# Three small edits to a one-core decoder layer: where the gating bias lies, when it is turned, and where a quarter of x2 is staged

## The chip, the cores and the metric

The kernel runs on one core of a Trainium2 chip. TensorE (PE) multiplies matrices and writes to PSUM banks. VectorE (DVE), ScalarE (ACT) and GpSimd (POOL) do the element-wise work. SyncE (SP) and POOL issue the transfers between the chip's memory (HBM) and the on-chip buffer (SBUF). Every engine works through its own instructions in order, and semaphores make one engine wait for another or for a transfer.

The metric is the device time of one execution in microseconds. For the kernel before, three runs gave 1558.74, 1558.91 and 1561.43 us; the median is 1558.91.

## The reference, cut to what matters

The program is one layer of a decoder with 512 positions and 2048 channels, all in float32:

```
h  = RMSNorm(x);  proj = h @ w_in          # q, k, v, gates, z_a, u, v, z_b, merge logits
o_a = sparse_attention(q, k, v) * silu(z_a)
u, v = split(gelu(uv))
o_b = u * (tril(w_s) @ LayerNorm(v) + b_s) * silu(z_b)      # gMLP gating, 8 groups, chunks of 128
merged = sigmoid(m_a) * (o_a @ w_up_a) + sigmoid(m_b) * (o_b @ w_up_b)
x2 = x + merged @ w_out
x3 = x2 + sigmoid(x2 @ w_ple_gate) * (p @ w_ple)
out = RMSNorm(x3) * final_g
```

Two pieces matter here. The first is `b_s`, the bias of the spatial gating, an array of 8 groups by 128 positions (`sgu_b`), together with the 8 matrices `w_s` of 128 by 128 (`sgu_w`); both must be transposed before the gating can use them. The second is x2, the layer's residual stream after the output projection: it is produced with positions on the partitions, and the next product, `x2 @ w_ple_gate`, needs it transposed, with channels on the partitions.

## The kernel before

**Precision.** Every float32 operand is split into a high part, made by ACT (`high`, line 142 or 144), and a low part, made by DVE (`low`, line 148 or 150). Each product is then three matmuls: high by high, high by low, low by high (lines 355 to 357, and 393 to 395 for the plain jobs). Activations are split once; weights are split as they stream in.

**Jobs, granules and units.** The matmul work is a list of jobs, one for each block of weight columns: `u`, `vn`, `zb`, `m0` to `m3` (columns of `w_in`), `ua`, `ub` (up projections), `wo0` to `wo2` (output projection), `pg0`, `pg1`, `pg3` (the last gate). The generator `gemm` walks through them. It stops after every unit of a few matmuls; `fill(n)` runs n units, and `finish(name)` runs to the end of a job. Four units make one granule: 12 matmuls of 512 columns that use up one split piece of the weights. At the start of a granule `gemm` runs the deferred work (`flush`), splits the weights for two granules ahead (`split_to`, with `state["ahead"]` at 2), and takes work off a background list (`pop`).

**Kind "S" jobs** compute two column blocks at a time by a scheme that trades one product for sums of the operands. It has seven products, named "1" to "7". The weight quarters b11 and b12 have four places each, the other two quarters go through the three places of `raw`. The high and low parts of S jobs lie in `hs` and `ls`, three places each. Job `u` runs its products in the order 1, 2, 5, 6 and 3 alternating, 7, 4, with 4 granules for each product; its product "1" uses small pieces from another pool, so `hs` is first used by product "2", from the fifth granule on. The four b11 places form a ring (`ring(i, ...)`, tags b110 to b113), which also serves other short-lived tiles in stages when no b11 is there.

**The pace of background work.** `state["pops"]` is added to a running sum at every granule, and each whole number reached takes one item off the background list. The fraction that is left is carried on through the rest of the program. After the gating's matrices have been turned, 64 items in four chunks (`oa_chunk`) are put on the list; they prepare the attention output for the up projection and must be gone when job `vn` ends. Later lists are four `sum_chunk`s during `wo0` and `wo1` (pace 0.7), `x2_chunk`s during `pg0` (0.8), and two `s4_chunk`s during `pg1` (0.5).

**The stage around the first edits.** When attention ends, the pools `quad` (b12, hs, ls, s1) and `mix` are opened on its memory. Line 1374 loads the two halves of `sgu_w`, line 1375 loads the bias `bn`, both on POOL's queue. After job `za7` come 12 units of `u`, the transpose of the bias on PE (`ps_b`, line 1491) and its copy on DVE (line 1492), 4 units, then for each half of `sgu_w` four transposes (`ps_w`, line 1497), a multiplication by the triangle (line 1498), a store to DRAM (line 1500) and 4 units.

**The stage around the third edit.** After `wo0`, its 512 columns of x2 are turned in two pairs of 128-column blocks (`turn_x2(0, ...)`, line 1729). For each block `stage` (line 1720) splits the transposed block into a tile named `x2t` and stores that to DRAM (`x2t_d`). `third_sum` (line 1698 onwards) takes a difference of halves through a tile `third` in `hs` and a tile `stage` in `ls`, and stores it as `s3x_d`. All this runs beside the matmuls of `wo1`, 8 units after each pair. Job `wo2`, the next S job, loads its b11 quarter into the ring.

## Time and profile before

| What | Value |
|---|---|
| median of three runs | 1558.91 us |
| the profiled execution, its own time | 1559.0 us |
| its span, first to last instruction | 1557.3 us |
| mean granted TensorE clock | 0.997 of full speed |
| PE busy | 1538.7 us, 99% of the span |
| DVE busy | 1195.3 us, 77% |
| ACT busy | 785.0 us, 50% |
| POOL busy | 252.8 us, 16% |
| HBM traffic over the span | 172 GB/s |

How to read the rows that follow. A timeline row has the start in us from the span's start, the duration in us, the engine, the line, the operation, the tiles it writes and reads (out<-in), the shapes and a count; a bracket at its end tells how long the engine stood idle before it and whose end released it. A row of waits tells the waiting instruction, whom it waited for, the time in total, how often, and the longest. A row of stretches has the stretch, its length, each engine's busy time with its count, the granted clock, the share of the DMA engines and GB/s. A DMA row ends with KB each and the time from issue to landing.

### The profile page before, as it was taken

To read this page: it belongs to the slowest core of one execution; us is meant where nothing else is said; L and a number is where in the kernel's file an instruction comes from. 1 tells how busy PE (TensorE), PEld (TensorE's weight loads), DVE (VectorE), ACT (ScalarE), POOL (GpSimd) and SP (SyncE) were. 2 spreads that over 40 slices of the span, in tenths; PEclk is the share of its full clock that TensorE was granted. 3 is DMA by queue.
4 is the path that set the end of the run, shared out by engine and by line. 5 is a ranking of instruction groups with operands and counts; after the bars stand their busy time and mean duration, and the time that the engine had idled before them with its cause. 6 is when DMAs were issued, how large, how long until landed. Compare 5 with 4: busy or idle time off the path is not lost.

```text
span 1557.3 us, 20518 instructions
## 1 busy us (share of the span) xinstructions
PE 1538.7 (99%) x7438; PEld 1288.9 (83%) x7438; DVE 1195.3 (77%) x1869; ACT 785.0 (50%) x1345; POOL 252.8 (16%) x413
## 2 busy tenths in 40 slices
PE   9999999999999999999999999999999999999997
PEld 8889988888887888888888888888888878888886
DVE  6547758888886888978887777777665677878877
ACT  6434446667664555555545444455323344544456
POOL 1201101101122342201121212210131221000000
PEclk9999999999999999999999999999999999999999
DMA  8436731213226894826473737674833478454665
GB/s 322 127 81 195 222 80 50 59 51 109 75 74 211 240 307 136 250 68 230 142 258 112 265 104 253 234 260 170 298 121 95 136 219 268 149 201 164 189 202 190
DMA packets 161429, 269.23 MB, mean 173 GB/s; under 512 B 9752, under 2 KB 80048, under 8 KB 158768
## 3 DMA queue, kind: packets, MB, share of 16 engines
q1 hardware_dynamic: 116240, 151.67, 31.0%
q0 software_dynamic: 44944, 116.00, 22.5%
q8 instruction: 58, 0.95, 0.2%
q14 instruction: 43, 0.35, 0.1%
q10 hardware_dynamic: 144, 0.26, 0.0%
HBM read 209.69 MB, written 58.20 MB: 172 GB/s over the span
## 4 chain that ended last, share of the span: by engine, by line
PE 94%; DVE 3%; DMA 1%; ACT 1%; issue 1%; POOL 0%; DVEq 0%; POOLq 0%; ACTq 0%
PE ps_m L355 7%; PE ps_m L357 7%; PE ps_m L356 7%; PE ps_t L1204 2%; PE ps_ub L394 2%; PE ps_ub L393 2%; PE ps_ub L395 2%; PE ps_za L381 2%; PE ps_za L382 2%; PE ps_za L383 2%; PE ps_pg L356 2%; PE ps_wo L355 2%; PE ps_pg L357 2%; PE ps_ua L356 2%; PE ps_ua L355 2%; PE ps_zb L356 2%
## 5 line engine op out<-in xcount | busy, mean ns | idle before, releaser
L148 DVE TENSOR_TENSOR ls<-b,hs 128x1024 fp32r<-128x1024 f32 x196 | 239.9, 1224 | 116.1 <-ACT hs L142 114.8
L142 ACT CAST hs<-b 128x1024 fp32r<-128x1024 f32 x196 | 206.0, 1052 | 231.2 <-PE ps_m L357 87.7
L148 DVE TENSOR_TENSOR lo<-raw,hi 128x512 fp32r<-128x512 f32 (+1 forms) x216 | 151.4, 706 | 82.5 <-issue 21.3
L142 ACT CAST hi<-raw 128x512 fp32r<-128x512 f32 (+1 forms) x216 | 129.3, 606 | 150.5 <-PE ps_ub L395 46.4
L142 ACT CAST hs<-raw 128x1024 fp32r<-128x1024 f32 x80 | 84.2, 1054 | 94.4 <-PE ps_m L357 35.5
L148 DVE TENSOR_TENSOR ls<-raw,hs 128x1024 fp32r<-128x1024 f32 x80 | 97.8, 1223 | 14.8 <-ACT hs L142 14.6
L355 PE MATMUL ps_m<-hs,act_h 128*128 128x512 f32 x256 | 100.5, 393 | 0.0
L356 PE MATMUL ps_m<-ls,act_h 128*128 128x512 f32 x256 | 99.7, 389 | 0.0
L357 PE MATMUL ps_m<-hs,act_l 128*128 128x512 f32 x256 | 99.6, 389 | 0.0
L258 DVE TENSOR_TENSOR b<-raw,b 128x1024 f32<-128x1024 f32 x80 | 97.5, 1219 | 1.9 <-DMA raw<-in_w_in_dram 1.3
L258 DVE TENSOR_TENSOR b<-b,b 128x1024 f32<-128x1024 f32 x80 | 97.5, 1218 | 0.0
L142 ACT CAST pth<-ps_t 128x512 fp32r<-128x512 f32 (+1 forms) x88 | 47.9, 545 | 65.8 <-PE ps_t L1204 65.5
L1165 ACT ACTIVATE prob<-prob,st 128x512 f32<-128x512 f32 (+3 forms) x128 | 70.7, 556 | 4.0 <-DVE st L1156 3.8
L148 DVE TENSOR_TENSOR ptl<-ps_t,pth 128x512 fp32r<-128x512 f32 (+1 forms) x88 | 56.2, 639 | 21.0 <-ACT pth L142 20.0
L1156 DVE CUSTOM_DVE_ANT_0 prob<-ps_s,b 128x512 f32<-128x512 f32 (+3 forms) x128 | 56.3, 486 | 10.0 <-PE ps_s L1153 9.7
L357 PEld LDWEIGHTS ps_m<-hs,act_l 128*128 128x128 f32 x256 | 48.1, 188 | 10.1
L355 PEld LDWEIGHTS ps_m<-hs,act_h 128*128 128x128 f32 x256 | 48.1, 188 | 9.7
L356 PEld LDWEIGHTS ps_m<-ls,act_h 128*128 128x128 f32 x256 | 48.1, 188 | 9.7
L381 PE MATMUL ps_za<-act_h,hi 128*128 128x512 f32 x128 | 55.8, 436 | 0.0
L381 PE MATMUL ps_q<-act_h,hi 128*128 128x512 f32 x128 | 53.6, 419 | 0.0
L394 PE MATMUL ps_wo<-lo,act_h 128*128 128x512 f32 x128 | 49.9, 390 | 2.2 <-DVE lo L148 2.2
L1204 PEld LDWEIGHTS ps_t<-ident,prob 128*128 128x128 f32 x320 | 39.7, 140 | 13.8 <-DVE ptl L148 2.8
(641 smaller groups left out, 4395.9 us busy)
## 6 DMA issues: line engine op xcount, KB each, us to landing
raw<-in_w_in_dram SPq DMA_DIRECT2D x112, 512.0 KB, 3.9
b<-in_w_in_dram SPq DMA_DIRECT2D x56, 512.0 KB, 5.3
raw<-in_w_out_dram SPq DMA_DIRECT2D x24, 512.0 KB, 3.8
raw<-in_w_ple_gate_dram SPq DMA_DIRECT2D x24, 512.0 KB, 4.4
raw<-in_w_up_b_dram SPq DMA_DIRECT2D x16, 512.0 KB, 3.7
hsum<-h_stage POOLq DMA_DIRECT2D x12, 512.0 KB, 4.1
gate<-keep POOLq DMA_DIRECT2D x24, 256.0 KB, 4.7
oa_d<-oa_g POOLq DMA_DIRECT2D x40, 128.0 KB, 3.4
```

Of the source, the lines that this page charges most:

```text
L142: nc.scalar.copy(hi, src)
L148: nc.vector.tensor_tensor(out=lo, in0=src, in1=hi.bitcast(F32), op=ALU.subtract)
L258: nc.vector.tensor_tensor(out=b[o], in0=b[x], in1=b[y], op=ALU.subtract)
L355: nc.tensor.matmul(o, ah, wh, start=st, stop=False, skip_group_check=go)
L356: nc.tensor.matmul(o, ah, wl, start=False, stop=False, skip_group_check=go)
L357: nc.tensor.matmul(o, al, wh, start=False, stop=sp, skip_group_check=go)
L381: nc.tensor.matmul(ps, hi[:, j], ah, start=st, stop=False)
L382: nc.tensor.matmul(ps, hi[:, j], al, start=False, stop=False)
L394: nc.tensor.matmul(o, ah[:, sl], lo[:, j], start=False, stop=False)
L1156: nc.vector.tensor_tensor_reduce(out=pt[:, j * n:j * n + n], in0=o[:, j], in1=b0[:, 512 - n:], scale=-SLOPE[h], scalar=3.0e38, op0=ALU.add ...
L1165: nc.scalar.activation(sl, sl, AF.Exp, bias=st[:, 0, j, hh:hh + 1], scale=-1.0, accum_out=st[:, 1, j, hh:hh + 1])
L1204: nc.tensor.transpose(b[:, (2 * e + hh) * P:(2 * e + hh + 1) * P], pts[hh][:, c:c + P], ident)
```

## The change

There are three edits.

1. The bias tile `bn` moves from the tag `s1` (two places, otherwise used for sums and for what product "1" leaves) to the tag `hs` (three places).
2. The bias is turned after 20 units of `u` instead of 12, so it and all that follows it in the program (the two halves of `sgu_w`, the start of the background chunks) come two granules later. The pace of the background goes from 1.3 to 1.33 items for each granule.
3. The four `x2t` tiles, one for each 128-column block of x2's first quarter, lie in the four places of the b11 ring instead of in `hs`.

```
-    bn = quad["pool"].tile([P, 2, 256], F32, tag="s1", name="bn", bufs=2).rearrange("p a s -> p (a s)")[:8, :P]
+    bn = quad["pool"].tile([P, 2, 256], F32, tag="hs", name="bn", bufs=3).rearrange("p a s -> p (a s)")[:8, :P]
...
-    state["pops"] = 1.3
-    fill(12)
+    state["pops"] = 1.33
+    fill(20)
     b = bank("o", "ps_b")
     nc.tensor.transpose(b[:, :8], bn, ident[:8, :8])
...
     def stage(k, b):
-        o = quad["pool"].tile([P, 2, S], F32R, tag="hs", name="x2t", bufs=3)
+        o = ring(k, F32R)
         split(o[:, 0], o[:, 1], b, later=True)
         deferred.append(lambda: nc.gpsimd.dma_start(x2t_dram[:, :, k], o))
```

The function that the new line calls stands in the kernel already:

```
    def ring(i, dtype, n=2):
        return quad["ring"].tile([P, n, S], dtype, tag=f"b11{i}", name="b11")
```

## The prediction

> **What bounds the kernel now.** I read the profile from the whole to the place: the page first, then PE's own waits, then the timeline where these waits fall. The first two lines are the page's busy time and its chain; the next two are PE's two longest waits.

> ```profile
> PE 1538.7 (99%) x7438; PEld 1288.9 (83%) x7438; DVE 1195.3 (77%) x1869; ACT 785.0 (50%) x1345; POOL 252.8 (16%) x413
> PE 94%; DVE 3%; DMA 1%; ACT 1%; issue 1%; POOL 0%; DVEq 0%; POOLq 0%; ACTq 0%
> PE ps_b L1491 <- DMA bn<-in_sgu_b_dram: 2.8, 1, 2.8
> PE ps_wo L394 <- DVE lo L148: 2.2, 1, 2.2
> ```

> PE is the bound, and it almost never waits. So only what touches a PE wait can move the time, and the two longest belong to the bias and to the stage of `wo1`, exactly where the edits are. Each is now sized from PE's timeline.

> ```profile
> 489.60 0.39 PE L355 MATMUL ps_u<-hi,act_h 128*128 128x512 f32 x1
> ...
> 497.54 0.39 PE L357 MATMUL ps_u<-hi,act_l 128*128 128x512 f32 x1
> 500.72 0.19 PE L1491 MATMUL ps_b<-ident,bn 8*128 8x8 f32 x1 [2.79 <-DMA bn<-in_sgu_b_dram]
> 500.84 0.50 PE L355 MATMUL ps_u<-hi,act_h 128*128 128x512 f32 x1
> 501.18 0.40 PE L356 MATMUL ps_u<-lo,act_h 128*128 128x512 f32 x1
> ...
> 504.95 0.97 PE L1497 MATMUL ps_w<-ident,wn 128*128 128x128 f32 x4
> 505.66 0.50 PE L355 MATMUL ps_u<-hs,act_h 128*128 128x512 f32 x1
> ...
> 508.50 0.60 PE L1497 MATMUL ps_w<-ident,wn 128*128 128x128 f32 x4
> 508.85 0.48 PE L355 MATMUL ps_u<-hs,act_h 128*128 128x512 f32 x1
> ```

> From the start of `u` at 489.60 to the 36th matmul at 497.54, matmuls follow each other every 7.94/35 = 0.227 us. The next would have begun at 497.77; `ps_b` begins at 500.72. **Loss A is 2.95 us.** Then the stretch view shows something more:

> ```profile
> 498.00:501.00 3.00, 0.28 (x2) 0.29 (x3) 1.45 (x3) 0.00 (x0) 0.00 (x0) 1.00 1.04 401
> 501.00:506.00 5.00, 5.00 (x18) 3.95 (x18) 2.39 (x3) 1.40 (x4) 0.07 (x1) 0.66 0.81 275
> 506.00:512.00 6.00, 6.00 (x30) 4.96 (x29) 5.84 (x6) 1.96 (x3) 3.38 (x7) 1.00 0.76 250
> ```

> The granted clock (third column from the end) is 0.66 in the five microseconds behind the wait, and 1.00 around them. On the timeline: the granule from 500.84 should take 12 x 0.227 = 2.72, plus 0.11 for the slower first step behind a transpose (501.18 - 500.84 is 0.34), and end at 503.67; the four transposes come at 504.95, 1.28 late. They take 0.71 (505.66 - 504.95) where the next four take 0.35 (508.85 - 508.50), 0.36 more. **Loss B is 1.64 us**; the clock column gives 5 x 0.34 = 1.7, which agrees.

> The other wait, in `wo1`:

> ```profile
> 1270.70 0.59 ACT L142 CAST x2t<-ps_x 128x512 fp32r<-128x512 f32 x1 [6.33 <-DMA x2t_d<-x2t]
> 1266.81 0.69 DVE L148 TENSOR_TENSOR stage<-third,stage 128x512 fp32r<-128x512 f32 x1
> 1272.60 1.29 DVE L148 TENSOR_TENSOR x2t<-ps_x,x2t 128x512 fp32r<-128x512 f32 x2 [5.11 <-ACT third L1698]
> 1274.46 0.68 DVE L148 TENSOR_TENSOR lo<-raw,hi 128x512 fp32r<-128x512 f32 x1
> 1272.60 0.39 PE L393 MATMUL ps_wo<-hi,act_h 128*128 128x512 f32 x1
> 1275.20 0.50 PE L394 MATMUL ps_wo<-lo,act_h 128*128 128x512 f32 x1 [2.21 <-DVE lo L148]
> ```

> The third `x2t` piece finds no `hs` place until the first one's store has landed. ACT stands 6.33 us, DVE behind it 5.11, and the low part of a weight piece, next in DVE's order, comes too late for PE. The matmul due at 1272.83 starts at 1275.20, and its first step is 0.11 longer, as above. **Loss C is 2.48 us.**

> **The change, part by part.** Edit 2 moves PE's transposes (1 + 8), DVE's copy and two multiplications, two stores on POOL, and the 64 background items by two granules. Nothing is added or taken away, so every instruction keeps its price; what changes is who waits.

> *The bias.* It is turned after 60 matmuls: 489.60 + 60 x 0.227 = 503.2. Has it landed by then?

> ```profile
> L1375 POOL DMA_DIRECT2D bn<-in_sgu_b_dram x1: 582/582/582, 491.9 to 491.9; - x1
> DMA to landing us min/median/max: 8.6/8.6/8.6
> 492.51 1.83 POOL L570 TENSOR_TENSOR o<-o,zt 128x256 f32<-128x256 f32 x2
> 495.77 2.00 ACT L142 CAST hs<-raw 128x1024 fp32r<-128x1024 f32 x2
> 508.70 1.05 ACT L142 CAST hs<-raw 128x1024 fp32r<-128x1024 f32 x1 [1.88 <-PE ps_u L357]
> 509.78 1.23 DVE L148 TENSOR_TENSOR ls<-raw,hs 128x1024 fp32r<-128x1024 f32 x1
> ```

> Its issue stays where it is on POOL's queue, so it lands at 491.9 + 8.6 = 500.6, with 2.6 us to spare. Loss A goes, and loss B with it, since no gap is left: -4.59. What is late next? The `sgu_w` halves were loaded ahead of the bias, and are turned still later.

> *The place.* In `hs` the bias now holds one of three places until 503.2. The tile `zt` (read by POOL until 492.51 + 1.83 = 494.3) takes one, the first weight piece of product "2" the third, the second piece (the second cast of the row at 495.77) follows into `zt`'s place. The third piece's cast must wait for the end of the fifth granule, about 503.4, like the cast at 508.70 that waits for PE. Its 1.05, and DVE's 1.23 behind it, end at 505.7. PE wants the low part at 503.3 + 2.72 + 0.11 + 0.35 + 0.34 = 506.8. So the cover is 1.1 us; bounds 0 and 2.3 (cast and low part in the open), I take 0, for the piece is nearest to the covered rows. The `s1` place that becomes free served nobody: the tiles that product "1" leaves did not wait for it.

> *The queues.* POOL's order changes.

> ```profile
> 510.67 1.08 POOL L1393 DMA_DIRECT2D oa_f<-o_d  x2
> 516.93 1.51 POOL L724 DMA_DIRECT2D act_h<-h_d  x2
> 523.80 0.63 ACT L144 ACTIVATE oa_g<-oa_f 128x512 fp32r<-128x512 f32 x1
> ```

> The two `oa_f` loads fall behind the four `h_d` loads, and ACT wants the first result four granules later, some 11 us; with landings of 9 us that is tight. ACT may stand there 1 to 2 us, but weights are split two granules (5.4 us) ahead at 2.3 us each, which covers it. SP's queue is not passed by anything. Cost 0, bound 2.

> *The pace.* `u`, `vn` and `zb` have 84 granules: 84 x 1.3 = 109.2, 84 x 1.33 = 111.72. The list empties one granule later (the last but one of `vn` before, the last after), and a fraction of 0.72 instead of 0.2 is carried on. So `sum_chunk` and `x2_chunk` items come up to one granule sooner, and the `s4_chunk` items in `pg1` one later. There PE waits for DVE's low parts:

> ```profile
> 1446.69 0.39 PE L355 MATMUL ps_pg<-hs,p_l 128*128 128x512 f32 x1
> 1446.96 0.50 PE L356 MATMUL ps_pg<-ls,p_l 128*128 128x512 f32 x1
> ```

> PE loses 0.15 us (0.04 late, then 0.11). The items move away from the granules that also hold a weight sum, so this may vanish; or it may grow by one item, two of DVE's 0.69. Between -0.15 and +1.4 I take 0.

> *The four places.* With `x2t` in the ring, ACT makes the third and fourth piece as soon as PE has turned them, about 1265.5, and loss C goes: -2.48. The next who waits is a tile `stage` in `ls`, one granule sooner by the pace: it wants the place whose store is this one.

> ```profile
> s3x_d<-stage POOLq DMA_DIRECT2D x1, 256.0 KB, 6.5
> x2t_d<-x2t POOLq DMA_DIRECT2D x2, 512.0 KB, 9.2
> ```

> That store follows the DVE row at 1266.81 and lands about 1274.3. ACT then needs 0.6 for `stage` and 0.6 for the next weight piece, DVE 0.7: 1276.3. PE, unbroken, needs that piece two granules after 1272.60, at 1278.2. Cover 1.9; bounds 0 and 2.5, I take 0.

> **The sum.** -2.95 - 1.64 - 2.48 = -7.07. The profiled execution took 1559.0 (span 1557.3 and 1.7 around it), which becomes 1551.9; the median of the runs, 1558.91, is 0.1 lower and gives 1551.8. I say 1551.9.

> [...] The clock row comes first: the gap between 497.8 and 500.7 is 2.95 us, and half clock follows (0.34 lost of five us is 3.4 us at half). [...]

> **The rivals.**
> 1. *The clock halves there whatever the gap.* Loss B stays: 1551.9 + 1.6 = 1553.5. [...]
> 2. *The bias holds back the second piece.* If that gets the bias's place instead of `zt`'s, its low part is ready at 505.7 and wanted at 503.7: 2.0 idle, and up to 1.6 of half clock. 1553.9 to 1555.5. Against it: `zt` is read to its end by 494.3, before the cast.
> 3. *The wait in `wo1` comes back through `ls`* (the 1.9 of cover are gone if the store lands 2 us later): up to 2.5 back, 1554.4.
> 4. *The transfers do not follow.* Around 498 to 501 the DMA engines are full (1.04, 401 GB/s). If PE, 4.6 us earlier, only meets weights that have not landed, both gains are given back, 1559. Against it: PE has no wait on a weight's DMA.
> 5. *Slower: the ring holds up `wo2`.* SP's queue is in order, and the third b11 load needs the third `x2t` store landed.

> ```profile
> 1282.47 1.74 SPq L230 DMA_DIRECT2D b<-in_w_out_dram  x3
> b<-in_w_out_dram SPq DMA_DIRECT2D x8, 512.0 KB, 10.9
> 1302.31 0.39 PE L355 MATMUL ps_wo<-hs,act_h 128*128 128x512 f32 x1
> ```

> `wo2` would start 7.1 before 1302.3, at 1295.2, and want that piece four granules on, 1306.1; landing 10.9 and splitting 2.3 before it, the load must be issued by 1292.9. Each microsecond beyond costs one; from 1300.0 the kernel is slower than before, from 1303.1 by over 0.2%: 1562. Against it: the stores leave about 1269, and with the 9.2 us of the row above that ends at 1278.

> **Chances.** Forecast 0.64, rivals in their order 0.04, 0.08, 0.08, 0.09, 0.07. The first four cases are all faster by over 0.2% (below 1555.8; 0.2%, 3.1 us, is about what a measurement of this kernel can tell from no change): 0.84. Same 0.09, slower 0.07. The forecast's own range is 1551.4 to 1553.3 (pg1's 0.15 gone, or its 1.4 added); the range reaches over rivals 1 to 3, 1551.0 to 1556.0.

> **What would show it.** No PE wait at `ps_b`, clock 1.00 from 500 to 510, the bias's transpose near 503.2; no wait of ACT on `x2t_d`, no wait of PE at `ps_wo`; `wo2` starting 7 us sooner. Wrong steps would show as: PE waiting for `ls` in `u` between 503 and 507 (place), ACT waiting for `s3x_d` with PE waiting behind it (ls), ACT waiting for `oa_f` (queue), new waits in `pg1` (pace), SP waiting for `x2t_d` past 1293 (ring).

## The result and the profile after

The changed kernel takes 1551.66 us (median of four runs, 1551.45 to 1551.81). The kernel before, timed beside it, has a median of 1559.83 (1558.74 to 1561.43). The ratio is 0.9947, with a 95% interval of 0.9929 to 0.9964. The forecast was 1551.9. The profiled execution of the changed kernel took 1551.8, with a span of 1550.1 where the kernel before had 1557.3: 7.2 us less, against a sum of 7.07.

So the total was right. The experiments below show that its parts were not all where the prediction put them.

The page of the changed kernel, busy time and chain:

```profile
PE 1536.1 (99%) x7438; PEld 1287.8 (83%) x7438; DVE 1194.6 (77%) x1869; ACT 785.4 (51%) x1345; POOL 251.4 (16%) x413
PE 96%; DVE 2%; ACT 1%; issue 0%; POOL 0%; DVEq 0%; POOLq 0%; ACTq 0%
```

PE's longest waits in the changed kernel (the waiting line, whom it waited for, us in total, times, longest):

```profile
PE ps_spin L947 <- POOL eps_t L87: 1.4, 1, 1.4
PE ps_t L1204 <- DVE ptl L148: 1.3, 1, 1.3
PE ps_pl L389 <- ACT hi L142: 0.8, 1, 0.8
PE ps_u L355 <- DVE keep L695: 0.4, 1, 0.4
```

The two waits of 2.8 and 2.2 us are gone, and no new one of that size has come. The stretches around the old wait in the changed kernel (the third column from the end is the granted clock):

```profile
498.00:501.00 3.00, 3.00 (x15) 2.49 (x14) 3.00 (x4) 0.95 (x2) 0.00 (x0) 1.00 1.04 403
501.00:506.00 5.00, 5.00 (x23) 3.90 (x22) 2.18 (x3) 2.19 (x4) 1.38 (x3) 1.00 1.08 418
506.00:512.00 6.00, 6.00 (x32) 4.95 (x32) 5.97 (x7) 2.42 (x4) 0.56 (x1) 1.00 1.04 410
```

PE is busy throughout, and the clock stays at 1.00 where it was 0.66. How much each place gave is read from single matmuls that both kernels run at the same position of PE's order. First the timeline of PE in the kernel before, then in the changed one; the three rows lie behind the gating's transposes, behind the wait in `wo1`, and behind the late piece in `pg1`:

```profile
516.70 0.39 PE L356 MATMUL ps_u<-ls,act_h 128*128 128x512 f32 x1
1275.54 0.39 PE L395 MATMUL ps_wo<-hi,act_l 128*128 128x512 f32 x1
1447.30 0.40 PE L357 MATMUL ps_pg<-hs,p_l 128*128 128x512 f32 x1
```

```profile
512.21 0.39 PE L356 MATMUL ps_u<-ls,act_h 128*128 128x512 f32 x1
1268.56 0.39 PE L395 MATMUL ps_wo<-hi,act_l 128*128 128x512 f32 x1
1440.14 0.39 PE L357 MATMUL ps_pg<-hs,p_l 128*128 128x512 f32 x1
```

The distances are 4.49, 6.98 and 7.16 us. Losses A and B together gave 4.49 (forecast 4.59), the wait in `wo1` gave 6.98 - 4.49 = 2.49 (forecast 2.48), and `pg1` gave 0.18 (forecast 0, between 0.15 less and 1.4 more).

### The profile page after: what moved, and what is told of

Same layout as the page of the kernel before. It is cut to its first block, busy times and chain, and to the rows that moved or that the text cites. A ratio compares the mean times of both kernels' runs of the same rounds, so it can differ in the third digit from the quotient of the medians.

```text
span 1550.1 us, 20517 instructions
## 1 busy us (share of the span) xinstructions
PE 1536.1 (99%) x7438; PEld 1287.8 (83%) x7438; DVE 1194.6 (77%) x1869; ACT 785.4 (51%) x1345; POOL 251.4 (16%) x413
## 4 chain that ended last, share of the span: by engine, by line
PE 96%; DVE 2%; ACT 1%; issue 0%; POOL 0%; DVEq 0%; POOLq 0%; ACTq 0%
PE ps_m L355 7%; PE ps_m L357 7%; PE ps_m L356 7%; PE ps_za L381 2%; PE ps_t L1204 2%; PE ps_za L382 2%; PE ps_za L383 2%; PE ps_ub L393 2%; PE ps_ub L394 2%; PE ps_wo L394 2%; PE ps_ub L395 2%; PE ps_wo L395 2%; PE ps_wo L393 2%; PE ps_wo L356 2%; PE ps_wo L355 2%; PE ps_pg L356 2%
## 5 line engine op out<-in xcount | busy, mean ns | idle before, releaser
L148 DVE TENSOR_TENSOR ls<-b,hs 128x1024 fp32r<-128x1024 f32 x196 | 239.7, 1224 | 116.1 <-ACT hs L142 115.0
L142 ACT CAST hs<-b 128x1024 fp32r<-128x1024 f32 x196 | 206.1, 1052 | 231.3 <-PE ps_m L357 88.0
L148 DVE TENSOR_TENSOR lo<-raw,hi 128x512 fp32r<-128x512 f32 (+1 forms) x216 | 151.6, 706 | 81.8 <-issue 26.1
L142 ACT CAST hi<-raw 128x512 fp32r<-128x512 f32 (+1 forms) x216 | 129.3, 606 | 138.6 <-PE ps_ub L395 48.5
L142 ACT CAST hs<-raw 128x1024 fp32r<-128x1024 f32 x80 | 84.2, 1054 | 98.4 <-PE ps_m L357 35.5
L148 DVE TENSOR_TENSOR ls<-raw,hs 128x1024 fp32r<-128x1024 f32 x80 | 97.8, 1222 | 17.2 <-ACT hs L142 17.0
L355 PE MATMUL ps_m<-hs,act_h 128*128 128x512 f32 x256 | 100.5, 393 | 0.0
L356 PE MATMUL ps_m<-ls,act_h 128*128 128x512 f32 x256 | 99.7, 389 | 0.0
L357 PE MATMUL ps_m<-hs,act_l 128*128 128x512 f32 x256 | 99.7, 389 | 0.0
L142 ACT CAST pth<-ps_t 128x512 fp32r<-128x512 f32 (+1 forms) x88 | 48.0, 545 | 65.8 <-PE ps_t L1204 65.4
L148 DVE TENSOR_TENSOR ptl<-ps_t,pth 128x512 fp32r<-128x512 f32 (+1 forms) x88 | 56.2, 639 | 21.0 <-ACT pth L142 20.0
L357 PEld LDWEIGHTS ps_m<-hs,act_l 128*128 128x128 f32 x256 | 48.1, 188 | 10.1
L356 PEld LDWEIGHTS ps_m<-ls,act_h 128*128 128x128 f32 x256 | 48.1, 188 | 9.7
L355 PEld LDWEIGHTS ps_m<-hs,act_h 128*128 128x128 f32 x256 | 48.1, 188 | 9.7
L1204 PE MATMUL ps_t<-ident,prob 128*128 128x128 f32 x320 | 49.5, 273 | 1.4 <-DVE ptl L148 1.3
## 6 DMA issues: line engine op xcount, KB each, us to landing
raw<-in_w_in_dram SPq DMA_DIRECT2D x112, 512.0 KB, 3.8
b<-in_w_in_dram SPq DMA_DIRECT2D x56, 512.0 KB, 5.8
raw<-in_w_out_dram SPq DMA_DIRECT2D x24, 512.0 KB, 4.1
raw<-in_w_ple_gate_dram SPq DMA_DIRECT2D x24, 512.0 KB, 3.9
raw<-in_w_up_b_dram SPq DMA_DIRECT2D x16, 512.0 KB, 3.7
hsum<-h_stage POOLq DMA_DIRECT2D x12, 512.0 KB, 4.0
gate<-keep POOLq DMA_DIRECT2D x24, 256.0 KB, 4.1
```

The source lines that it names most:

```text
L142: nc.scalar.copy(hi, src)
L148: nc.vector.tensor_tensor(out=lo, in0=src, in1=hi.bitcast(F32), op=ALU.subtract)
L355: nc.tensor.matmul(o, ah, wh, start=st, stop=False, skip_group_check=go)
L356: nc.tensor.matmul(o, ah, wl, start=False, stop=False, skip_group_check=go)
L357: nc.tensor.matmul(o, al, wh, start=False, stop=sp, skip_group_check=go)
L1204: nc.tensor.transpose(b[:, (2 * e + hh) * P:(2 * e + hh + 1) * P], pts[hh][:, c:c + P], ident)
```

## The experiments

The theory going in was the prediction's own: three separate losses, each removed by its own edit. The first four kernels take the change apart.

**Bias alone.** The first two edits, with the third undone:

```
-        o = ring(k, F32R)
+        o = quad["pool"].tile([P, 2, S], F32R, tag="hs", name="x2t", bufs=3)
```

> The first two edits alone; the x2t tiles stay in hs. Theory of three separate losses: PE's wait at the bias and the half clock behind it go, 4.5 us, and the 0.2 us in pg1 goes with the pace; the wait at ps_wo stays at 2.2 to 2.5 us. Time 4.7 us under the kernel before, about 1554.2 against a profiled 1559.0. Rival, the edits hang together: the pace moves a sum's tile in front of the x2t casts, and the wait at ps_wo changes by a microsecond or more either way.

Measured: 1552.14 us (1551.71 to 1552.30), ratio 0.9948 (0.9936 to 0.9961). The theory's 1554.2 is missed by 2 us: without the ring the kernel is as fast as the whole change, within 0.5 us, and the span of the profiled execution is 1550.0 against 1550.1. PE has no wait at `ps_wo`. ACT, on its timeline, still waits for an `x2t` store, but briefly:

```profile
1262.38 1.07 ACT L142 CAST x2t<-ps_x 128x512 fp32r<-128x512 f32 x2 [2.55 <-DMA x2t_d<-x2t]
```

Where ACT stood 6.33 us before, it now stands 2.55, and what is behind it is still in time for PE. The place is the same; the store comes back sooner.

**Ring alone.** The third edit on the kernel before:

```
-        o = quad["pool"].tile([P, 2, S], F32R, tag="hs", name="x2t", bufs=3)
+        o = ring(k, F32R)
```

> The third edit alone. Theory of three separate losses: PE's wait at ps_wo goes, 2.45 us, and nothing else moves; the wait at ps_b (2.8) and the half clock behind it stay: about 1556.5. Rival, it is the pace and not the ring that removes the wait at ps_wo: then this kernel still shows a wait of 1 to 2.5 us there and takes 1557.5 to 1559.

Measured: 1556.43 (1554.70 to 1558.10), ratio 0.9977 (0.9967 to 0.9986). No wait at `ps_wo`; the wait at `ps_b` is 2.8 as before. The ring by itself does what the prediction said.

**Pace alone.** One number in the kernel before:

```
-    state["pops"] = 1.3
+    state["pops"] = 1.33
```

> Only the pace goes from 1.3 to 1.33. If the pace by itself moves the items away from the full granules of pg1, the step of 0.15 to 0.18 us at the row that was 1446.96 goes, and the waits at ps_b and ps_wo stay as they are: 0.2 us less, under what a comparison of times can tell, so the trace decides. Rival: the pace alone also changes the wait at ps_wo (2.2 before), by up to 1.2 us either way.

Measured: 1556.44 (1554.53 to 1557.91), ratio 0.9978 (0.9969 to 0.9987). This was expected to be worth 0.2 us and is worth as much as the ring: the wait at `ps_wo` is gone here too, and ACT waits 2.20 us for the store. The rival's half (that the pace changes this wait) held, and by twice its size. So the wait in `wo1` was removed twice by the change, once by the ring and once by the pace.

**The place of the bias.** The changed kernel with the bias back in `s1`:

```
-    bn = quad["pool"].tile([P, 2, 256], F32, tag="hs", name="bn", bufs=3)...
+    bn = quad["pool"].tile([P, 2, 256], F32, tag="s1", name="bn", bufs=2)...
```

> The changed kernel with the bias back in s1 (the second and third edit without the first). ACT's second copy of a result of product 1 then waits for the bias's place until 503.4, about 2.3 us, and the cast of the third piece follows at about 504.0, its low part at 506.4; PE wants it at 506.9. Theory that the place in itself is worth nothing: same time as the changed kernel, 1551.7, with ACT waiting and PE not. Rival, the place matters: PE waits for ls near 507 by 0.5 us or more, and the time is 1552.2 to 1553.

Measured: 1551.82 (1551.68 to 1552.47). On its ACT timeline the second copy of a result now waits for the bias to be turned, and the third piece's cast comes behind it:

```profile
503.57 0.59 ACT L682 COPY keep<-ps_u 128x512 f32<-128x512 f32 x1 [2.96 <-PE ps_b L1491]
504.14 2.03 ACT L142 CAST hs<-raw 128x1024 fp32r<-128x1024 f32 x2
```

DVE's low part starts at 505.23 and takes 1.23, to 506.46; PE, which wants it at about 507, does not wait. The first edit is worth nothing that the times show: 0.2 us, less than the runs of either kernel scatter.

**What the bias waited for, and the clock.** The next four kernels change only the wait at `ps_b`. In the first the load of the bias goes ahead of the two halves of `sgu_w`:

```
+    nc.gpsimd.dma_start(bn, sgu_b)
     for hf in range(2):
         nc.gpsimd.dma_start(wn[hf], ...)
-    nc.gpsimd.dma_start(bn, sgu_b)
```

> The kernel before with one thing changed: the load of the bias is issued ahead of the two sgu_w halves, 1.5 us sooner, and nothing is turned later. Theory that PE's loss at the bias is only the landing of a small load behind two large ones: it lands between 497.5 and 499, PE waits 0 to 1.1 us instead of 2.8, no half clock follows, and the time falls by 3.4 to 4.6 us. Rival, all loads of this stretch share full DMA engines and land together: it lands at about 499.5 to 500.5 as before, and the time falls by under 1 us, unless the half clock goes.

Measured: 1556.62 (1555.20 to 1557.08), ratio 0.9977 (0.9968 to 0.9986), 3.7 us less than the 1560.27 beside it. PE's timeline shows the wait cut to a quarter:

```profile
498.63 0.20 PE L1491 MATMUL ps_b<-ident,bn 8*128 8x8 f32 x1 [0.74 <-DMA bn<-in_sgu_b_dram]
```

It lands about 2.1 us sooner (500.58 before, 498.50 here), within what the theory named. But 1.5 us of that is the earlier issue (491.94 before, 490.41 here). From issue to landing the load still takes 8.1 us, where it took 8.6 behind the two halves, so standing behind them explains about 0.5 us of its landing; where the other 8.1 go was not tested.

In the other three the bias is turned one unit later, one unit sooner and four units sooner; the halves of `sgu_w` stay in place:

```
-    fill(12)
+    fill(13)        # 11 and 8 in the other two
...
     nc.vector.tensor_copy(sgu_bt, b[:, :8])
-    fill(4)
+    fill(3)         # 5 and 8
```

> The kernel before with the bias turned one unit (3 matmuls, 0.68 us) later, the sgu_w halves where they were. PE's gap should be 2.95 - 0.68 = 2.3 us. Theory that the half clock answers a gap of some length, with the limit between 2.4 and 2.95: no half clock, and the time falls by 0.7 + 1.6 = 2.3 us. Rival, any gap here sets it off: 0.7 us less only.

> The kernel before with the bias turned one unit sooner: PE's gap should be 2.95 + 0.68 = 3.6 us. If the half clock is of fixed length (3.4 us), the loss behind the gap stays at 1.6 to 1.7 and the time rises by 0.7 us; if it grows with the gap, by 1 us or more.

> The kernel before with the bias turned four units sooner: PE's gap should be 2.95 + 2.72 = 5.7 us. With one half-clock stretch of 3.4 us the time rises by 2.7 us; if a gap this long costs a second stretch, by 4.4 us.

Measured: 1557.86 (ratio 0.9990, 0.9981 to 0.9999), 1561.34 (1.0008, 0.9999 to 1.0017) and 1562.80 (1.0021, 1.0011 to 1.0030). So 2.4 us less, 1.1 more and 2.5 more than the 1560.27 beside them, against 2.3 less, 0.7 or 1 more, and 2.7 or 4.4 more; the interval of the second includes no change at all. In one profiled execution of each, the clock behind the gap is at half for no stretch in the first kernel, for two of 3.41 us in the second and for one in the third; the last two have another half window behind the wait in `wo1`. That the first kernel's median meets the forecast is chance: its ten runs spread from 1556.0 to 1560.1, with mean clocks from 0.998 down to 0.996, so half clock did not go in all of them.

So in these runs the length of the gap alone does not decide it. In the trace of the kernel before, the granted clock goes to half at 502.30, back to full at 505.71, 3.413 us later, and to half again at 1550.19, 1044.48 us on, 306 times as long. Windows of that length do not lie alike in every trace: with the ring alone, a kernel that is the same up to `wo1`, the half clock begins at 500.76 and not at 502.30. Cut along such windows, the stretches of four kernels follow. Each row has the window, its length, PE's busy time first among the engines, and the granted clock. The kernel before, the window with the gap and the next, then the two windows that share the gap in `wo1` and the next:

```profile
498.88:502.30 3.42, 1.58 (x7) 1.35 (x8) 1.87 (x4) 0.00 (x0) 0.00 (x0) 1.00 1.05 407
502.30:505.71 3.41, 3.41 (x12) 2.65 (x11) 1.09 (x1) 1.10 (x3) 0.00 (x0) 0.50 0.79 248
1270.30:1273.71 3.41, 2.69 (x12) 1.88 (x10) 1.11 (x2) 2.59 (x6) 0.12 (x1) 1.00 0.68 217
1273.71:1277.12 3.41, 1.92 (x8) 1.61 (x9) 3.38 (x8) 1.44 (x4) 2.71 (x4) 1.00 0.79 243
1277.12:1280.53 3.41, 3.41 (x16) 2.81 (x15) 3.38 (x6) 1.92 (x4) 0.67 (x1) 1.00 1.01 245
```

The bias turned one unit later, a wait of 2.0 us at `ps_b`:

```profile
496.94:500.35 3.41, 1.73 (x8) 1.11 (x6) 3.41 (x4) 0.89 (x1) 0.00 (x0) 1.00 1.04 402
500.35:503.76 3.41, 3.06 (x16) 2.60 (x17) 1.50 (x4) 1.15 (x3) 0.00 (x0) 1.00 1.05 407
```

The load of the bias first, a wait of 2.0 us too, this time at `ps_wo`:

```profile
1269.10:1272.51 3.41, 1.45 (x6) 1.05 (x6) 3.41 (x8) 1.98 (x4) 2.78 (x4) 1.00 0.56 180
1272.51:1275.92 3.41, 3.41 (x9) 2.65 (x8) 3.34 (x6) 1.76 (x3) 0.07 (x1) 0.50 1.01 240
```

The bias turned four units sooner:

```profile
493.65:497.06 3.41, 1.60 (x8) 0.98 (x6) 1.87 (x2) 2.40 (x4) 1.94 (x5) 1.00 1.04 352
497.06:500.48 3.42, 0.09 (x1) 0.12 (x1) 0.00 (x0) 0.73 (x1) 0.00 (x0) 1.00 1.04 401
500.48:503.89 3.41, 3.41 (x9) 2.71 (x10) 0.78 (x3) 0.00 (x0) 0.00 (x0) 0.50 0.39 150
```

In these rows a window at full clock in which PE is busy for 0.09, 1.45 or 1.58 us is followed by one at half clock, and a window with 1.60 or more is not. (One window of 1.58 us, shown in the last section, is not followed by half clock either.) By these rows the difference lay in how much of one gap fell into one window. The same wait of 2.0 us left PE 1.45 us of work in a window of one kernel, which cost a half window, and 1.73 us in the other, which cost nothing.

**The phase in `wo1`.** Two questions were left: why the pace removes the wait, and whether the ring is then worth anything. The pace leaves a fraction behind (0.2 before, 0.72 after), so the items of `wo0` and `wo1` fall into other granules. The next three kernels set only this fraction, ahead of `wo0`. Bias alone with the old fraction:

```
     state["pops"] = 0.7
+    state["due"] -= 0.52
```

> The first two edits alone, with the fraction that the pace leaves behind put back to 0.2 ahead of wo0 (the running sum less 0.52), so that from there on the background items come in the granules of the kernel before. Theory that the wait in wo1 hangs on the phase of the items: the wait at ps_wo comes back (2 to 2.4 us, PE), ACT waits for x2t_d 6 us again, and the time is 1554 to 1556, some 2.5 to 3.5 us over the same kernel with its own phase (1552.1). Rival, what removed the wait was PE's earlier arrival and not the phase: no wait at ps_wo, 1552.3.

Measured: 1554.55 (1554.27 to 1556.46), ratio 0.9970 (0.9958 to 0.9981), 2.4 us over the same kernel with its own fraction (a little under the 2.5 to 3.5 expected). The wait is back, in PE's waits and on ACT's timeline:

```profile
PE ps_wo L394 <- DVE lo L148: 2.3, 1, 2.3
```

```profile
1266.26 0.59 ACT L142 CAST x2t<-ps_x 128x512 fp32r<-128x512 f32 x1 [6.26 <-DMA x2t_d<-x2t]
```

The changed kernel with the same line:

> The changed kernel with the same 0.52 taken from the running sum ahead of wo0: the ring, but the phase of the kernel before. Theory that the ring or the phase alone is enough: no wait at ps_wo, and 1551.8 to 1552.1 (the 0.18 us in pg1 are back). Rival, the ring needs the phase: a wait at ps_wo of 0.5 us or more, over 1552.3.

Measured: 1552.01 (1551.96 to 1552.59), no wait at `ps_wo`. At the old phase the ring is worth 1554.55 - 1552.01 = 2.5 us; at the new phase it is worth 1552.14 - 1551.66 = 0.5 by the medians, which the spans (1550.0 and 1550.1) do not confirm.

The kernel before with `state["due"] += 0.52` at that place:

> The kernel before, pace 1.3, with 0.52 added to the running sum ahead of wo0 and nothing else. Theory of the phase: it does what the pace of 1.33 did, no wait at ps_wo, the bias's wait and the half clock as in the kernel before: 1556.0 to 1556.8. Rival, the pace works through something in u, vn or zb: the wait at ps_wo stays and the time is that of the kernel before, about 1559.8.

Measured: 1555.78 (1554.29 to 1558.10), ratio 0.9976 (0.9966 to 0.9985), no wait at `ps_wo`, the wait at `ps_b` 2.6. So the pace works through the fraction that it leaves for `wo0` and `wo1`; nothing in the jobs it was set for is needed.

Last, what the phase changes there. On POOL's timeline of the kernel before, the item that stores `s_d` stands directly ahead of the store of x2's first quarter:

```profile
1258.34 0.72 POOL L1459 DMA_DIRECT2D s_d<-stage  x1 [2.82 <-DVE stage L148]
1259.05 0.77 POOL L1678 DMA_DIRECT2D x_d<-x  x1
1261.59 1.38 POOL L1723 DMA_DIRECT2D x2t_d<-x2t  x2 [1.76 <-DVE x2t L148]
```

POOL waits 2.82 us for the item's data; `x_d`, a transfer of 1 MB whose own data are ready at 1256.8, leaves behind it, 2.5 us ahead of the `x2t` stores. In the kernel with the pace alone the item comes sooner, `x_d` waits only for its own data, and it leaves 5.2 us ahead of them:

```profile
1253.70 0.72 POOL L1459 DMA_DIRECT2D s_d<-stage  x1 [1.24 <-DVE stage L148]
1256.09 0.77 POOL L1678 DMA_DIRECT2D x_d<-x  x1 [1.67 <-DVE x L815]
1261.27 1.38 POOL L1723 DMA_DIRECT2D x2t_d<-x2t  x2 [4.41 <-DVE x2t L148]
```

The last kernel moves that store out of POOL's order and leaves the phase alone:

```
-        nc.gpsimd.dma_start(columns(x2_dram, cg), x_tiles[cg])
+        (nc.gpsimd if cg else nc.sync).dma_start(columns(x2_dram, cg), x_tiles[cg])
```

> The kernel before with one transfer moved: the store of x2's first quarter (x_d, 1 MB) is issued by SP, so that it needn't stand behind the s_d store in POOL's order. Theory that x_d, issued 2.5 us ahead of the x2t stores, is what makes these land in 9 us instead of 5: x_d leaves at about 1256.5, the x2t stores land in 5 to 6.5 us, ACT waits for them 2 to 3.5 instead of 6.3 us, PE waits at ps_wo 0 to 0.3, and the time falls by 2 to 3.4 us. Rival, the x2t stores are slow for the weights' load beside them (raw, 1259.27): they still land in 8 to 9 us, and the wait at ps_wo stays at 1.5 us or more. A mishap would be SP held up by x_d and the weight load behind it late.

Measured: 1556.13 (1554.41 to 1557.07), ratio 0.9975 (0.9965 to 0.9985), no wait at `ps_wo`. That is 3.6 us less, slightly more than the 2 to 3.4 expected. The transfers around it, first in the kernel before, then with the new pace, then with the store on SP (KB each, us from issue to landing):

```profile
x_d<-x POOLq DMA_DIRECT2D x1, 1024.0 KB, 7.3
x2t_d<-x2t POOLq DMA_DIRECT2D x2, 512.0 KB, 9.2
```

```profile
x_d<-x POOLq DMA_DIRECT2D x1, 1024.0 KB, 4.7
x2t_d<-x2t POOLq DMA_DIRECT2D x2, 512.0 KB, 5.1
```

```profile
x_d<-x SPq DMA_DIRECT2D x1, 1024.0 KB, 4.0
x2t_d<-x2t POOLq DMA_DIRECT2D x2, 512.0 KB, 5.9
```

With the large store out of the way the `x2t` stores land in 5.9 us instead of 9.2, without a new place and without a new pace. The weights' load that the rival named still leaves 2.3 us ahead of them (1257.08 here, 1259.27 before), so by itself it is not the cause. In the kernel before, `x_d` is under way until about 1266, beside both stores; in the other two it has landed (at 1260.8 and 1258.7) before they leave. Whether the transfers hinder each other in POOL's queue or in the DMA engines, these runs do not separate. The chain of loss C is therefore: an item's store delays `x_d` in POOL's order, `x_d` then runs beside the `x2t` stores, these land late, the third `x2t` piece waits for its place, and DVE and PE wait behind it. The ring cuts it at the place, the pace at its first link.

The kernels that differ in bias, phase or ring at a glance (medians in us):

| Bias turned late | Phase | Ring | Median | Kernel |
|---|---|---|---|---|
| no | old | no | 1559.7 to 1560.3 | before |
| no | old | yes | 1556.43 | ring alone |
| no | new | no | 1556.44, 1555.78 | pace alone; fraction alone |
| yes | old | no | 1554.55 | bias alone, old fraction |
| yes | old | yes | 1552.01 | change, old fraction |
| yes | new | no | 1552.14 | bias alone |
| yes | new | yes | 1551.66, 1551.82 | the change; with the bias in `s1` |

## Why the prediction was right, and where it was not

*Loss A* went as worked out. The changed kernel's PE timeline:

```profile
503.26 0.23 PE L1491 MATMUL ps_b<-ident,bn 8*128 8x8 f32 x1
503.41 0.50 PE L355 MATMUL ps_u<-hs,act_h 128*128 128x512 f32 x1
...
506.95 0.39 PE L356 MATMUL ps_u<-ls,act_h 128*128 128x512 f32 x1
```

The bias is turned at 503.26 (forecast 503.2) without a wait.

*Loss B* went with it, and rival 1, that the clock halves there whatever the gap, is refuted by the clock of 1.00 in the changed kernel. The expectation for the bias turned one unit later took the length of the gap for what decides, 2.4 us in `wo1` without half clock and 2.95 us here with it; by the windows the difference lay in where the gaps fell. PE was busy for 2.69 and 1.92 us in the two windows that share the gap in `wo1`, and for 1.58 us in the one ahead of the half clock, where 1.84 us of 3.42 were idle.

*The place.* The third piece's cast was put at 503.4, its low part at 505.7 and PE's need at 506.8. In the changed kernel, ACT's cast and DVE's low part:

```profile
503.36 1.05 ACT L142 CAST hs<-raw 128x1024 fp32r<-128x1024 f32 x1 [2.04 <-PE ps_u L357]
504.44 1.23 DVE L148 TENSOR_TENSOR ls<-raw,hs 128x1024 fp32r<-128x1024 f32 x1 [2.82 <-ACT hs L142]
```

The low part ends at 505.67 and PE uses it at 506.95: a cover of 1.28 where 1.1 was forecast. Rival 2 did not come.

*The queues.* The `oa_f` loads fell behind the four `h_d` loads, as said, and ACT took the first result without a wait, so the cost is 0. It was tighter than forecast: 8.4 us lie between issue and use, not 11, and the loads landed in 7.2 and not 9. The POOL and ACT rows of the changed kernel:

```profile
516.82 1.16 POOL L1393 DMA_DIRECT2D oa_f<-o_d  x2
525.17 0.63 ACT L144 ACTIVATE oa_g<-oa_f 128x512 fp32r<-128x512 f32 x1
```

*The pace* is the step that failed. The prediction said that `sum_chunk` items come up to one granule sooner, and priced that only for a tile in `ls` and for `pg1`. It did not follow the item's store on POOL's queue, which holds up `x_d` behind it: with the pace alone `s_d` leaves at 1253.70 instead of 1258.34, and `x_d` at 1256.09 instead of 1259.05. A term that was put at 0 took away the whole of loss C (kernels with the pace alone and the fraction alone). In `pg1` its size was 0.18 less instead of 0.

*The four places.* "With `x2t` in the ring, loss C goes" is true, and the kernel with the ring alone shows it. That the ring is what takes it away in the changed kernel is not: there the loss would have gone without it. The sum came out right because loss C stood in it once, whichever edit removed it; that the effect which the prediction missed fell on the same wait, and not on another, was luck. The sentence on the next wait was wrong as well: the tile `stage` does not wait for its place. On ACT's timeline of the changed kernel it carries no wait:

```profile
1266.40 0.62 ACT L142 CAST stage<-whole 128x512 fp32r<-128x512 f32 x1
```

DVE makes the first difference 5.8 us sooner, at 1261.04 instead of 1266.81, and not only because PE is 4.5 us earlier: two `whole` rows and one `s` row of a background item, which lay ahead of it in the kernel before, are done by then. Its store leaves at 1262.02 and lands in 3.9 us instead of 6.5, at 1265.9, half a microsecond before ACT's row at 1266.40; rival 3 did not come. DVE's row:

```profile
1261.04 0.68 DVE L148 TENSOR_TENSOR stage<-third,stage 128x512 fp32r<-128x512 f32 x1
```

*Rivals 4 and 5.* No weight was late, and SP's first six b11 loads went out from 1272.31 without a wait for `x2t_d`, far from the 1292.9 at which it would have cost something. SP's and PE's rows of the changed kernel:

```profile
1272.31 4.96 SPq L230 DMA_DIRECT2D b<-in_w_out_dram  x6
1295.31 0.39 PE L355 MATMUL ps_wo<-hs,act_h 128*128 128x512 f32 x1
```

`wo2` starts at 1295.31 instead of 1302.31, 7.0 us sooner (forecast 7).

*The base.* The sum was set against one execution of 1559.0. The medians of the kernel before, measured later, are 1559.7 to 1560.3, so by the medians the change is worth about 8 us and not 7. The profiled execution had half clock behind one of its two gaps. The 32 runs of the kernel before that stand beside the kernels with the bias turned sooner or later fall into 13 with a mean clock of 0.997 (1558.3 to 1559.7 us) and 19 with 0.996 or 0.995 (1560.0 to 1561.2). The bias alone with the old fraction has one gap left, the one in `wo1`, and its seven runs lie at 1554.3 to 1554.6 and at 1556.1 to 1556.5; the profiled one, of 1556.14, has the half window behind that gap. That the second group of the kernel before has half clock behind both gaps would fit this but was not seen in a trace of it. The lower end of the forecast's own range, 1551.4, does not come out of its terms (1551.9 less 0.15 is 1551.75); the measured 1551.66 lies between the two.

What stays open: whether the ring is worth anything at the new phase (0.5 us by the medians, nothing by the spans), why the load of the bias takes 8 us to land, and by which resource `x_d` slows the `x2t` stores.

## What to carry to other kernels

When an edit shifts a schedule, follow every item that it moves onto every queue it issues to, and ask which large transfer now leaves beside which small one: here a change of pace by 0.03 let one store leave 4.6 us sooner and was worth as much as a new buffer. If two edits may each remove the same wait, count it once and say that either will do; only a kernel with one edit at a time tells which did. Here a wait of PE of 2 to 3 us cost up to 1.7 us more than itself in some executions (1.64 behind the 2.8 us at `ps_b` in the kernel before) and not in others (clock of 1.00 behind the 2.0 us there with the bias turned one unit later), so one profile of a kernel with such waits was one draw.

## What the runs showed of the hardware

```profile
495.97:499.38 3.41, 1.58 (x7) 0.97 (x6) 2.96 (x3) 1.43 (x2) 0.00 (x0) 1.00 1.04 398
499.38:502.80 3.42, 2.67 (x12) 2.26 (x13) 2.43 (x3) 0.17 (x1) 0.00 (x0) 1.00 1.05 389
```

- With the bias turned one unit sooner, a window at half clock with PE busy for 2.60 us was followed by another at half clock; in the kernel before, the one at half clock with 3.41 us busy was followed by full clock. The first rests on one trace; its rows are:

```profile
500.14:503.55 3.41, 2.60 (x7) 2.12 (x8) 2.32 (x3) 0.00 (x0) 0.00 (x0) 0.50 0.94 364
503.55:506.96 3.41, 3.41 (x10) 2.64 (x9) 0.12 (x1) 0.31 (x1) 0.00 (x0) 0.50 0.52 165
```

- Kernels without such a gap scatter by 0.4 to 0.8 us over their runs, those with one or two by 1.9 to 6 us.
